# Low parts of some weight blocks from an accumulating DMA instead of VectorE, in a float32 decoder block

## The chip, the cores and the metric

The kernel runs on one core of one Trainium2 chip. The metric is the device time of one execution in microseconds (us).

## The reference

One decoder layer over 256 tokens with 2048 channels, all in float32:

```
h = x + 1/2 * SwiGLU_1(RMSNorm(h))                       d_ff = 5632
u = RMSNorm(h); proj = u @ W_in                           2048 -> 7168
    8 heads of a gated linear recurrence (HGRN2), and 8 channel groups of a short convolution
h = h + W_out(concat(group norms of both))
h = h + 1/2 * SwiGLU_2(RMSNorm(h))                       d_ff = 5632
h = h + sigmoid(RMSNorm(h) @ W_pg) * (p @ W_pe)
y = RMSNorm_final(h)
```

Nearly all of the work is in the weight matrices of the two feed-forward parts, of W_in, W_out and W_pg.

## The kernel before

**Two parts.** TensorE multiplies in the type float32r, which keeps fewer bits than float32. So each weight and each activation is kept as a high part (its float32r rounding) and a low part (what is left), and a product is made of three terms: high by high, high by low, low by high. `product` (L103) does this for one 128 x 128 weight block with two matmuls: the low part of the weights by the high part of 256 tokens, and the high part of the weights by both parts of the activations (512 columns). But for the first of an accumulation, the low part comes first (L106, then L107; for the first L107, then L109).

**Steps.** All weights pass through a list of 360 steps, each a block of at most 16 weight blocks of 128 x 128 (1 MB; 32 of the down steps have 12 blocks). Step numbers: 0 to 87 are gate and up of the first feed-forward by turns, 88 to 135 its down projection (three steps a column block, of 16, 16 and 12 weight blocks), 136 to 207 the mixer (W_in, then W_out), 208 to 295 gate and up of the second feed-forward, 296 to 343 its down projection, 344 to 359 the gate of the embedding.

**A step's weights.** `load` (L93) brings a step's weights into a buffer `raw` (three of them, RAW_BUFS) by a DMA that SyncE (SP) issues (L85). `split` (L98) takes the block in two halves of 8 (or 6) weight blocks each. For each half `split_piece` lets ScalarE (ACT) write the high part `hi` with an activation Copy (L90), and then VectorE (DVE) the low part `lo` = raw - hi (L91). There are four `hi` and four `lo` buffers of half a step each, so the parts of two steps are there at a time.

**Order.** The loop at L747 issues, for each step i: the load of step i + 3, the split of step i + 2, the matmuls of step i, its epilogue (L131 to L150, or L191 for a down step), and hooks of the mixer. A framework adds all semaphores and puts the instructions of each engine into one in-order queue, near to this program order. So the split of step i + 2 waits until the matmuls of step i are done with the same half of its `hi` and `lo` buffers; and the load of step i + 3 waits until the split of step i has read the buffer `raw` that it takes. Only the start (L712) has an order by hand. GpSimd (POOL) does nothing but a few memsets: constants, and in the mixer L278 and L288.

Of the kernel before, what the change touches and what calls it, by code (L numbers as in the profile page):

```python
# [7 lines left out]
F32 = mybir.dt.float32  # L8
F32R = mybir.dt.float32r
I32 = mybir.dt.int32  # L10
AF = mybir.ActivationFunctionType
ALU = mybir.AluOpType
PSUM = bass.MemoryType.PSUM

P = 128
T = 256            # tokens
T2 = 2 * T
NB = 16            # 128-wide blocks of d_model
NF = 44            # 128-wide blocks of d_ff
NH = 8             # heads, conv groups  # L20
EPS = 1e-6
MAGIC = float(0x5F3759DF)
STAGES = (2, 8, 32)  # each joins four blocks of this many tokens
HW = 2 * NH        # heads x windows of 128 tokens
NM = 64 + 192 * len(STAGES)

# columns of the packed per-channel vectors
C_FFN1, C_MIX, C_FFN2, C_PLE, C_FIN = 0, 16, 32, 48, 64
C_HN, C_CN, C_CW, C_LB, C_SEL, C_ID = 80, 81, 89, 113, 129, 139
NCST = C_ID + P  # L30
# [4 lines left out]


class Step:
    """One block of at most 16 x [128, 128] weights and what is done with it."""

    def __init__(self, src, nk, mm, epi=None):  # L40
        self.src, self.nk, self.mm, self.epi = src, nk, mm, epi
# [5 lines left out]
def kernel(  # L47
# [3 lines left out]
    nc = tc.nc  # L51
    V, A, TE = nc.vector, nc.scalar, nc.tensor
# [5 lines left out]

    hT = const.tile([P, NB, T], F32, name="hT")
    xs = const.tile([P, NB, T2], F32R, name="xs")  # L60
    cst = const.tile([P, NCST], F32, name="cst")
    ones = const.tile([P, P], F32, name="ones")
    ones_r = const.tile([P, P], F32R, name="ones_r")
    sel = const.tile([P, 2 * P], F32R, name="sel")
    acc = const.tile([P, T], F32, name="acc")
    rb = const.tile([P, T], F32, name="rb")
    rt = const.tile([P, 2], F32, name="rt")
    lb = const.tile([P, NH], F32, name="lb")
    oml = const.tile([P, NH], F32, name="oml")
    ident = cst[:, C_ID:C_ID + P]  # L70

    def tt(shape=(P, T), dtype=F32, tag="t", bufs=6):
        return tmp.tile(list(shape), dtype, tag=tag, name=tag, bufs=bufs)

# [1 line left out]
    def new_raw(s):  # L76
        s.raw = wpool.tile([P, NB, P], F32, tag="raw", name="raw", bufs=RAW_BUFS)

    def new_parts(s):
        s.half = s.nk // 2  # L80
        s.parts = [tuple(wpool.tile([P, NB // 2, P], F32R, tag=t, name=t) for t in ("hi", "lo"))
                   for _ in range(2)]
# [4 lines left out]
    def split_piece(s, a, b):  # L87
        hi, lo = s.parts[a // s.half]
        r, sl = s.raw[:, a:b, :], slice(a % s.half, a % s.half + b - a)
        A.activation(hi[:, sl, :], r, AF.Copy)  # L90
        V.tensor_tensor(lo[:, sl, :], r, hi[:, sl, :].bitcast(F32), ALU.subtract)  # L91
# [4 lines left out]
            load_piece(s, i * s.nk // n, (i + 1) * s.nk // n)  # L96

    def split(s):  # L98
        new_parts(s)
        for k0 in (0, s.half):  # L100
            split_piece(s, k0, k0 + s.half)

    def product(hi, lo, m, ps, first, last):  # L103
        """ps[:, :T] += hi.x_hi; ps[:, T:] += hi.x_lo + lo.x_hi"""
        if not first:
            TE.matmul(ps[:, T:], lo, m[:, :T], start=False, stop=False)  # L106
        TE.matmul(ps, hi, m, start=first, stop=last)  # L107
        if first:
            TE.matmul(ps[:, T:], lo, m[:, :T], start=False, stop=False)  # L109

    def product_one(hi, lo, m, ps, first, last):
        """ps[:, :T] += all three"""
        TE.matmul(ps[:, :T], lo, m[:, :T], start=first, stop=False)  # L113
        TE.matmul(ps[:, :T], hi, m[:, T:], start=False, stop=False)  # L114
        TE.matmul(ps[:, :T], hi, m[:, :T], start=False, stop=last)  # L115
# [11 lines left out]
    def new_ps():  # L127
        return psum.tile([P, T2], F32, tag="ps", name="ps")

# [1 line left out]
    def halves(ps):  # L131
        t = tt()
        A.activation(t, ps[:, T:], AF.Copy)  # L133
# [41 lines left out]
    def row_scale():  # L175
        ps = new_ps()
        TE.matmul(ps[:, :T], ones, acc, start=True, stop=True)
        v = tt()
        V.tensor_scalar(v, ps[:, :T], 1.0 / (NB * P), EPS, ALU.mult, ALU.add)
        rsqrt(rb, v)  # L180
# [4 lines left out]
    def token_scale(ps):  # L185
        v = tt(shape=(P, 2), tag="v2", bufs=1)
        for i in range(2):
            V.tensor_scalar(v[:, i:i + 1], ps[i][:, 0:1], 1.0 / (NB * P), EPS, ALU.mult, ALU.add)
        rsqrt(rt, v)
# [11 lines left out]
        prep(j, c_gain)  # L201
        square_sum(j)

# [1 line left out]
    steps = []  # L205

    def at(i, f):
# [14 lines left out]
    def ffn(wg, wu, wd, c_next):  # L222
# [13 lines left out]
        i0 = len(steps)  # L236
        for f in range(NF):
            add(wg[f], NB, *gemm_in(g_epi))
            add(wu[f], NB, *gemm_in(u_epi(f)))

        def open_hid(s):
            st["pool"] = ExitStack()
            pool = st["pool"].enter_context(tc.tile_pool(name="hidp", bufs=1))
            st["hid"] = pool.tile([P, NF, T2], F32R, name="hid")

# [14 lines left out]
        steps[-1].after = close_hid  # L260
        return i0

# [1 line left out]
    def mixer():  # L264
        i0 = len(steps)
        m = {}
# [1 line left out]
        def open_mix(s):  # L268
            st["pool"] = ExitStack()
            m1 = st["pool"].enter_context(tc.tile_pool(name="mix1", bufs=1))  # L270
            m["Y"] = m1.tile([P, NH, T], F32, name="Y")
            m["Q"] = m1.tile([P, NH, T], F32, name="Q")
            m["masks"] = m1.tile([P, NM], F32, name="masks")
# [6 lines left out]
            m2 = st["hg"].enter_context(tc.tile_pool(name="mix2", bufs=1))  # L280
            m["K"] = m2.tile([P, NH, T], F32, name="K")
            m["f"] = m2.tile([P, NH * T], F32, name="f")
            m["t12"] = m2.tile([P, NH * T // 8], F32, name="t12")
            m["tot"] = [m2.tile([P, NH * T // n], F32, name=f"tot{n}") for n in (*STAGES, P)]
            m["V"] = m2.tile([P, 2, NH, P], F32, name="V")
# [49 lines left out]
                V.tensor_tensor(windows(m["Q"][:, h, :]), q_of(h), windows(f), ALU.mult)  # L335
            return epi

        # Tokens are taken in blocks whose length grows. Within a block Q holds q_t times the decays
        # from the block's start through t, K holds k_s times those after s to the block's end, tot
        # the whole block's: a score between two blocks is then a product of rows, no factor of which  # L340
        # exceeds 1, and the blocks between come in with their tot.
        def pairs(a):
            return a.rearrange("p (b two) -> p b two", two=2)

# [55 lines left out]
        def stage_scores(si, h):  # L400
            L = STAGES[si]
            nb = P // (4 * L)
# [44 lines left out]
            return d  # L447

        def stat(key, g, d, first, last):
            """rows g and NH + g: the sum over the group's channels"""  # L450
            if first:
                st[key] = new_ps()
            e = sel[:, P - g:2 * P - g]
            TE.matmul(st[key][:, :T], e, d[:, :T], start=first, stop=False)
            TE.matmul(st[key][:, :T], e, d[:, T:], start=False, stop=last)

        def stat_done(key):
            v = tt()
            V.tensor_scalar(v, st[key][:, :T], 1.0 / P, EPS, ALU.mult, ALU.add)
            r = tt()  # L460
            rsqrt(r, v)
            # rows g hold the high parts, rows NH + g the low ones
            rs = st["rs", key] = m["m1"].tile([P, T], F32R, tag="rs", name="rs", bufs=2)
            A.activation(rs, r, AF.Copy)
            V.tensor_scalar(r, r, cst[:, C_SEL + 9:C_SEL + 10], None, ALU.mult)
            V.scalar_tensor_tensor(rs, rs.bitcast(F32), cst[:, C_SEL + 8:C_SEL + 9], r, ALU.mult, ALU.add)
# [4 lines left out]
            st["nr" + key, g] = d  # L471

        def norm(key, g, t):
            """t (in place) times its group's scale"""
            ps = new_ps()
            TE.matmul(ps[:, :T], ones_r, st["nr" + key, g], start=True, stop=True)
            V.tensor_tensor(t, ps[:, :T], t, ALU.mult)
# [45 lines left out]
        g0 = len(steps)  # L523
# [14 lines left out]
        k = c0 + 3  # L538
# [25 lines left out]
        for h in range(NH):  # L564
            at(k + 2 + h // 2, lambda h=h: norm_rows("o", h))
            at(k + 3 + h // 2, lambda h=h: norm("o", h, m["Q"][:, h, :]))
        assert k + 3 < g0  # a head's norm comes before its gate

        def conv_out(key, c):
            y = m["Y"][:, c, :]  # L570
# [3 lines left out]
        for c in range(NH):  # L574
            key = "y0" if c < 4 else "y1"
# [20 lines left out]
        steps[-1].after = close_mix  # L596
        return i0

# [1 line left out]
    def ple():  # L600
        i0 = len(steps)
        m = st["ple"] = {}
# [84 lines left out]
    scale_at = {i_f1 + 4, i_mix, i_f2, i_ple}  # L687
    late = []

# [1 line left out]
    # the first gate and up blocks side by side, so that both go on while x comes in  # L691
    nc.sync.dma_start(cst, cst_d)
    for i in range(2):
        steps[i].src = w_first[i]
# [17 lines left out]
    with tc.manual_schedule():  # L712
        for a, b in pieces:
            s = steps[a // 8]
# [15 lines left out]
        V.tensor_tensor(acc, acc, rb, ALU.add)  # L730

    def prologue():
        # the lower bound of the forget gate: the softmax's first row
        mx, e0, e1 = (tt(shape=(P, NH), tag="lbt", bufs=3) for _ in range(3))
        l0, l1 = cst[:, C_LB:C_LB + NH], cst[:, C_LB + NH:C_LB + 2 * NH]
        V.tensor_tensor(mx, l0, l1, ALU.max)
        V.tensor_tensor(e0, l0, mx, ALU.subtract)
        V.tensor_tensor(e1, l1, mx, ALU.subtract)
        A.activation(e0, e0, AF.Exp)
        A.activation(e1, e1, AF.Exp)  # L740
        V.tensor_tensor(e1, e0, e1, ALU.add)
        V.reciprocal(e1, e1)
        V.tensor_tensor(lb, e0, e1, ALU.mult)
        V.tensor_scalar(oml, lb, -1.0, 1.0, ALU.mult, ALU.add)
# [23 lines left out]
        if s.after:  # L768
            s.after(s)

# [1 line left out]
    m = st["ple"]  # L772
    ps = st["ts"]
    token_scale(ps)
# [3 lines left out]
    ps = new_ps()  # L778
# [66 lines left out]
```

## Time and profile before

| | us |
|---|---|
| two executions | 2048.87 and 2050.26, median 2049.57 |
| span of the profiled execution | 2047.5 |
| TensorE busy (matmul) | 2028.2 |
| VectorE busy | 1373.2 |
| ScalarE busy | 1004.2 |
| GpSimd busy | 2.9 |

The span goes from the first to the last instruction of the program. The profile does not say which of the two executions it is from; its span lies 1.4 to 2.8 us under their times, 2.1 us under the median. PE is TensorE's matmuls, PEld its weight loads, DVE VectorE, ACT ScalarE, POOL GpSimd, SP SyncE. The ends of matmuls are modelled and overlap, so their mean durations are longer than the pace at which they follow each other. "L90" is line 90 of the kernel.

### The profile page before, as it was taken

Reading aid. Unit: us, or ns where it says so; the run is one execution under the profiler, and the core shown is the slowest. Engines: PE = TensorE matmul, PEld = TensorE weight load, DVE = VectorE, ACT = ScalarE, POOL = GpSimd, SP = SyncE. Lnnn points to the kernel's source line nnn. Section 1 sums busy time; section 2 is a strip of 40 time slices with the busy share of each in tenths; the row PEclk is TensorE's granted clock in tenths of the full one; section 3 lists DMA queues with packets and bytes.
Section 4 is the critical chain, followed back from the end, with each engine's and each line's share of the span. In section 5 each row is a group of like instructions: output and inputs, shape, how many; then the busy total and the mean of one; then the engine's idle time right before and its main releaser. Section 6 shows DMA issues by size and latency. Waiting matters only on the chain.

```text
span 2047.5 us, 29112 instructions
## 1 busy us (share of the span) xinstructions
PE 2028.2 (99%) x11630; PEld 1774.8 (87%) x11630; DVE 1373.2 (67%) x2131; ACT 1004.2 (49%) x1510; POOL 2.9 (0%) x7
## 2 busy tenths in 40 slices
PE   8999999999999999999999999999999999999997
PEld 7888888888888888888888888888888888888986
DVE  8766666666555565689798776666666665555686
ACT  7444444444444444543566544444444444444463
POOL 0000000000000000000000000000000000000000
PEclk9999999999999999999999999999999999999998
DMA  7555555555555555544455555555555555555642
GB/s 250 205 188 188 191 193 188 186 185 182 184 190 190 185 199 190 189 165 145 144 168 186 187 185 192 192 188 185 185 186 187 190 186 188 177 195 187 237 164 84
DMA packets 55720, 378.00 MB, mean 185 GB/s; under 512 B 6176, under 2 KB 6432, under 8 KB 13728
## 3 DMA queue, kind: packets, MB, share of 16 engines
q1 hardware_dynamic: 55584, 376.14, 53.8%
q8 instruction: 91, 1.49, 0.3%
q14 instruction: 45, 0.37, 0.1%
HBM read 374.02 MB, written 2.10 MB: 184 GB/s over the span
## 4 chain that ended last, share of the span: by engine, by line
PE 98%; DMA 1%; DVE 1%; SPq 0%; issue 0%; ACT 0%; DVEq 0%; ACTq 0%
PE ps L107 61%; PE ps L106 29%; PE ps L109 2%; PE ps L405 1%; PE ps L306 1%; PE ps L307 1%; PE ps L308 1%; PE ps L114 1%; PE ps L115 1%; PE ps L113 1%; DMA hT<-xT 0%; DMA raw<-w1g 0%; PE ps L352 0%; DVE hg L782 0%; PE ps L438 0%
## 5 line engine op out<-in xcount | busy, mean ns | idle before, releaser
L107 PE MATMUL ps<-xs,hi 128*128 128x512 f32 x3824 | 1330.7, 394 | 5.9 <-DVE xs L154 5.9
L91 DVE TENSOR_TENSOR lo<-raw,hi 128x1024 fp32r<-128x1024 f32 (+2 forms) x724 | 865.1, 1195 | 637.4 <-ACT hi L90 636.6
L90 ACT ACTIVATE hi<-raw 128x1024 fp32r<-128x1024 f32 (+2 forms) x724 | 750.2, 1037 | 981.3 <-PE ps L107 624.2
L106 PE MATMUL ps<-xs,lo 128*128 128x256 f32 x3585 | 1002.3, 280 | 0.3 <-DVE lo L91 0.3
L107 PEld LDWEIGHTS ps<-xs,hi 128*128 128x128 f32 x3824 | 704.4, 188 | 156.2 <-ACT hi L90 5.9
L106 PEld LDWEIGHTS ps<-xs,lo 128*128 128x128 f32 x3585 | 672.3, 188 | 11.6 <-DVE lo L91 0.8
L107 PE MATMUL ps<-hid,hi 128*128 128x512 f32 x1320 | 461.3, 393 | 0.0
L106 PE MATMUL ps<-hid,lo 128*128 128x256 f32 x1290 | 364.5, 283 | 0.0
L107 PEld LDWEIGHTS ps<-hid,hi 128*128 128x128 f32 x1320 | 245.9, 188 | 54.8
L106 PEld LDWEIGHTS ps<-hid,lo 128*128 128x128 f32 x1290 | 242.5, 188 | 1.5
L140 DVE TENSOR_TENSOR t<-t,rb 128x256 f32<-128x256 f32 x231 | 97.5, 424 | 6.6
L134 DVE TENSOR_TENSOR t<-ps,t 128x256 f32<-128x256 f32 x239 | 99.8, 418 | 0.2 <-ACT t L133 0.2
L133 ACT ACTIVATE t<-ps 128x256 f32<-128x256 f32 x239 | 87.1, 366 | 0.9 <-DVE rb L162 0.9
L107 PE MATMUL ps<-mixout,hi 128*128 128x512 f32 x240 | 83.6, 397 | 0.0
L109 PE MATMUL ps<-xs,lo 128*128 128x256 f32 x239 | 67.8, 284 | 0.1
L106 PE MATMUL ps<-mixout,lo 128*128 128x256 f32 x225 | 63.1, 281 | 0.0
L109 PEld LDWEIGHTS ps<-xs,lo 128*128 128x128 f32 x239 | 45.1, 189 | 10.1 <-DVE lo L91 1.0
L107 PEld LDWEIGHTS ps<-mixout,hi 128*128 128x128 f32 x240 | 44.1, 188 | 9.5
L145 ACT ACTIVATE s<-t 128x256 f32<-128x256 f32 x112 | 45.0, 402 | 0.6 <-DVE t L140 0.6
L106 PEld LDWEIGHTS ps<-mixout,lo 128*128 128x128 f32 x225 | 42.2, 188 | 0.9 <-ACT mixout L149 0.2
L232 DVE TENSOR_TENSOR t<-t 128x256 f32<-128x256 f32 x88 | 37.3, 424 | 2.9
L150 DVE TENSOR_TENSOR hid<-t,hid 128x256 fp32r<-128x256 f32 x88 | 36.7, 418 | 0.1
(177 smaller groups left out, 931.9 us busy)
## 6 DMA issues: line engine op xcount, KB each, us to landing
raw<-w_in SPq DMA_DIRECT2D x48, 1024.0 KB, 4.9
raw<-w2g SPq DMA_DIRECT2D x44, 1024.0 KB, 4.8
raw<-w2u SPq DMA_DIRECT2D x44, 1024.0 KB, 4.8
raw<-w1u SPq DMA_DIRECT2D x43, 1024.0 KB, 4.8
raw<-w1g SPq DMA_DIRECT2D x42, 1024.0 KB, 4.8
raw<-w1d SPq DMA_DIRECT2D x32, 1024.0 KB, 4.9
raw<-w2d SPq DMA_DIRECT2D x32, 1024.0 KB, 4.9
raw<-w_out SPq DMA_DIRECT2D x16, 1024.0 KB, 4.8
```

What stands on the lines that cost most here:

```text
L90: A.activation(hi[:, sl, :], r, AF.Copy)
L91: V.tensor_tensor(lo[:, sl, :], r, hi[:, sl, :].bitcast(F32), ALU.subtract)
L106: TE.matmul(ps[:, T:], lo, m[:, :T], start=False, stop=False)
L107: TE.matmul(ps, hi, m, start=first, stop=last)
L109: TE.matmul(ps[:, T:], lo, m[:, :T], start=False, stop=False)
L113: TE.matmul(ps[:, :T], lo, m[:, :T], start=first, stop=False)
L133: A.activation(t, ps[:, T:], AF.Copy)
L134: V.tensor_tensor(t, ps[:, :T], t, ALU.add)
L140: V.tensor_tensor(dst, t, rb, ALU.mult)
L145: A.activation(s, src, AF.Sigmoid)
L150: V.tensor_tensor(dst[:, T:], src, dst[:, :T].bitcast(F32), ALU.subtract)
L232: V.tensor_tensor(u, u, st["g"], ALU.mult)
```

## The change

In each step whose number leaves a remainder of 3 when divided by 4 (3, 7, ... 359: 90 steps), the second half gets its low part in another way. ScalarE writes `hi` as before, then a second activation writes `lo` = -hi; then a DMA issued by GpSimd adds `raw` onto `lo`. The first half of these steps, and both halves of all others, are split as before. Nothing else changes but that comments are taken out (line numbers ahead of `split` stay).

```diff
     def split(s):
         new_parts(s)
-        for k0 in (0, s.half):
-            split_piece(s, k0, k0 + s.half)
+        split_piece(s, 0, s.half)
+        if steps.index(s) % 4 != 3:
+            split_piece(s, s.half, s.nk)
+            return
+        hi, lo = s.parts[1]
+        r = s.raw[:, s.half:s.nk, :]
+        A.activation(hi[:, :s.half, :], r, AF.Copy)
+        A.activation(lo[:, :s.half, :], hi[:, :s.half, :].bitcast(F32), AF.Copy, scale=-1.0)
+        nc.gpsimd.dma_start(lo[:, :s.half, :], r, accum_op=ALU.add)
```

## Rows read from the trace of the kernel before

**Rows 1.** The page's engine part: busy us, share of the span, instructions.
```profile
PE 2028.2 (99%) x11630; PEld 1774.8 (87%) x11630; DVE 1373.2 (67%) x2131; ACT 1004.2 (49%) x1510; POOL 2.9 (0%) x7
```

**Rows 2.** The page's chain that ended last: share of the span by engine.
```profile
PE 98%; DMA 1%; DVE 1%; SPq 0%; issue 0%; ACT 0%; DVEq 0%; ACTq 0%
```

**Rows 3.** The waits of PE, whole span: us in total, times, longest.
```profile
PE ps L107 <- DVE xs L154: 5.9, 1, 5.9
PE ps L779 <- DVE t L777: 2.8, 1, 2.8
PE ps L183 <- ACT t L654: 1.5, 1, 1.5
...
```

**Rows 4.** Windows: busy us (instructions) by engine, granted PE clock, DMA share, GB/s.
```profile
1170.00:1675.00 505.00, 505.00 (x2899) 441.09 (x2898) 342.40 (x507) 244.48 (x364) 0.00 (x0) 1.00 0.55 188
```

**Rows 5.** Groups by shape, whole span: count | busy us, mean ns | idle before.
```profile
L90 ACT ACTIVATE hi<-raw 128x1024 fp32r<-128x1024 f32 x652 | 691.1, 1060 | 890.5 <-PE ps L107 542.9 <-issue 303.0 <-PE ps L308 23.0
...
L90 ACT ACTIVATE hi<-raw 128x768 fp32r<-128x768 f32 x64 | 54.2, 846 | 90.0 <-PE ps L107 81.3 <-PE ps L115 5.8 <-issue 2.9
...
L91 DVE TENSOR_TENSOR lo<-raw,hi 128x1024 fp32r<-128x1024 f32 x652 | 798.3, 1225 | 581.8 <-ACT hi L90 581.4
...
L91 DVE TENSOR_TENSOR lo<-raw,hi 128x768 fp32r<-128x768 f32 x64 | 61.3, 958 | 54.6 <-ACT hi L90 54.4
```

**Rows 6.** Groups of ACT in the first 197 us.
```profile
L90 ACT ACTIVATE hi<-raw 128x1024 fp32r<-128x1024 f32 (+1 forms) x74 | 74.6, 1012 | 83.0 <-PE ps L107 43.8 <-issue 35.9 <-DMA raw<-w1u 1.4
```

**Rows 7.** Timeline of ACT, 197 to 215: start us, us, what [idle before].
```profile
200.19 1.06 ACT L90 ACTIVATE hi<-raw 128x1024 fp32r<-128x1024 f32 x1 [1.45 <-PE ps L107]
201.16 0.36 ACT L133 ACTIVATE t<-ps 128x256 f32<-128x256 f32 x1
202.99 1.06 ACT L90 ACTIVATE hi<-raw 128x1024 fp32r<-128x1024 f32 x1 [1.47 <-issue]
...
205.80 1.06 ACT L90 ACTIVATE hi<-raw 128x1024 fp32r<-128x1024 f32 x1 [1.45 <-PE ps L107]
...
208.59 1.06 ACT L90 ACTIVATE hi<-raw 128x1024 fp32r<-128x1024 f32 x1 [1.46 <-issue]
...
214.20 1.06 ACT L90 ACTIVATE hi<-raw 128x1024 fp32r<-128x1024 f32 x1 [1.47 <-issue]
```

**Rows 8.** Timeline of PEld, 207.5 to 209: start us, us, what.
```profile
208.47 0.19 PEld L106 LDWEIGHTS ps<-xs,lo 128*128 128x128 f32 x1
```

**Rows 9.** Timeline of DVE, 199 to 209.
```profile
201.29 1.23 DVE L91 TENSOR_TENSOR lo<-raw,hi 128x1024 fp32r<-128x1024 f32 x1 [1.25 <-ACT hi L90]
...
202.43 0.42 DVE L134 TENSOR_TENSOR t<-ps,t 128x256 f32<-128x256 f32 x1
```

**Rows 10.** Timeline of SP's queue, 190 to 225.
```profile
202.54 0.33 SPq L85 DMA_DIRECT2D raw<-w1g  x1
208.14 0.33 SPq L85 DMA_DIRECT2D raw<-w1u  x1
```

**Rows 11.** Groups of ACT in the first 513 us.
```profile
L90 ACT ACTIVATE hi<-raw 128x1024 fp32r<-128x1024 f32 (+1 forms) x187 | 194.1, 1039 | 248.0 <-PE ps L107 127.1 <-issue 117.7 <-DMA raw<-w1u 1.4
```

**Rows 12.** Timeline of ACT, 512 to 524.
```profile
514.18 1.06 ACT L90 ACTIVATE hi<-raw 128x1024 fp32r<-128x1024 f32 x1 [1.75 <-PE ps L107]
...
521.13 0.84 ACT L90 ACTIVATE hi<-raw 128x768 fp32r<-128x768 f32 x1 [1.47 <-PE ps L107]
```

**Rows 13.** DMA issues: what, queue, count, KB each, median us from issue to landing.
```profile
raw<-w1u SPq DMA_DIRECT2D x43, 1024.0 KB, 4.8
...
wpe<-w_pe SPq DMA_DIRECT2D x2, 1024.0 KB, 7.7
...
out_dram<-hg SPq DMA_DIRECT2D x1, 512.0 KB, 2.8
```

**Rows 14.** Timeline of POOL, whole span (the longest of its instructions).
```profile
750.25 2.67 POOL L288 MEMSET S<- 128x3072 f32 x1
```

## The prediction

> **What bounds the kernel now.** I read the engines' busy times first: the matmuls are busy 99% of the span, VectorE 67%, ScalarE 49%, and GpSimd has seven instructions in all [rows 1]. A busy share alone can hide waits, so the chain of waits comes next: 98% of it is TensorE, VectorE and the DMAs have 1% each [rows 2]. TensorE's own waits agree: the three largest are 5.9, 2.8 and 1.5 us, one occurrence each [rows 3], together 10.2 us, all at the start or the end. Last the clock: in a long stretch of the second feed-forward it is 1.00, the level of 2.4 GHz, with TensorE busy for 505.00 of 505 us [rows 4]. So TensorE sets the end nearly everywhere, and work taken from VectorE is worth nothing by itself. What matters is whether the new way delivers the low part before TensorE asks for it.
>
> **What goes.** 90 subtractions on VectorE: 82 of 1.225 us in full steps and 8 of 0.958 us in the steps with 12 weight blocks [rows 5], 100.5 + 7.7 = 108 us of 1373. None of it is on the chain [rows 2]; I count 0.
>
> **What comes on ScalarE.** 90 negations. Their shapes are those of the high parts, so they cost what L90 costs: 82 x 1.060 + 8 x 0.846 = 94 us [rows 5], ScalarE then 1098 us, 54% of the span. What lies behind each in ScalarE's queue is seen at step 35, an affected one: 74 high parts stand before 197 us [rows 6], that is 8 small pieces of steps 0 and 1 and 2 x 33 halves of steps 2 to 34, so the row at 200.19 is the second half of step 35 [rows 7]. Behind it comes the epilogue's copy L133 (201.16), then the next high part at 202.99, before which ScalarE was idle for 1.47 us. A negation of 1.06 us fits into that idle time. L133 comes 1.06 us later, but VectorE, which then no longer does the subtraction of 1.23 us from 201.29 on, takes up the copy's result at about 202.6 instead of 202.43 [rows 9]: a delay of 0.2 us in an epilogue for which TensorE does not wait. Cost 0; without the idle time, 1.06 us of delay to a high part that has some 6 us in hand, so still 0.
>
> **What comes as a wait.** Now the low part of a second half lands by DMA, and the first matmul of that half (L106) waits for it; behind that one stands all of TensorE's queue, so a late landing costs its whole lateness, 1 for 1. The time in hand for step 35: the high part ends at 201.25; a hand-over between engines takes 0.04 us (VectorE starts at 201.29) [rows 7, 9], counted twice; with the negation that makes 201.25 + 0.04 + 1.06 + 0.04 = 202.39 for the issue. The high part at 208.59 is the first half of step 37, which may start when TensorE is done with the first half of step 35 [rows 7]; the weight load just before it, at 208.47 [rows 8], is where TensorE takes the low part of the second half. In hand: 208.47 - 202.39 = 6.1 us. I take this for 82 of the 90 steps.
>
> The other 8 follow a step of 12 weight blocks (every third affected step of the down projections), so TensorE comes round sooner. For step 91, the second half of which starts at 514.18 (187 high parts before 513 us [rows 11]: 8 + 2 x 89 + the first half of step 91), the issue is at 515.24 + 0.04 + 1.06 + 0.04 = 516.38 and the first half of step 93 at 521.13 [rows 12]; less the same 0.12 us, 521.01. In hand: 4.6 us.
>
> With X as the time from issue to landing: **time = 2049.6 + 82 x (X - 6.1 if above 0) + 8 x (X - 4.6 if above 0)**.
>
> **The size of X.** No row shows an accumulating DMA, or any DMA from GpSimd's queue. From below: 512 KB out of this memory take 2.8 us [rows 13]. From above: two loads of 1024 KB issued one behind the other take 7.7 us each [rows 13], and GpSimd's longest instruction is 2.67 us against 0.33 us of SP's issue [rows 10, 14]: were an issue on GpSimd that long, X = 7.7 + 2.67 - 0.33 = 10.0 us. The sum has two operands of 512 KB, so 1024 KB are read: the nearest row is the load of 1024 KB, 4.8 us from issue to landing [rows 13], and that is what I take. The 16 DMA engines are free for it: the load of the step before was issued 5.6 us earlier (208.14 - 202.54 is the spacing [rows 10]) and has landed after 4.8, and the next cannot go out before this DMA has read the buffer.
>
> At 4.8 us the 82 steps have 1.3 us to spare and the 8 lose 0.2 us each, 1.6 us in all.
>
> The Trainium skill has a price (DMA: Bandwidth & Descriptors, Anatomy of one DMA): about 2.0 us fixed and the bytes at 436 GB/s, for a DMA from GpSimd; no run here shows it. With both operands counted that is an estimate of 4.4 us, also inside both times in hand, and the sum would be 2049.6.
>
> **What moves.** The buffer `raw` is now held until the DMA has landed. The load of step 38, issued at 202.54 after VectorE's subtraction [rows 9, 10], goes out at 202.39 + 4.8 = 207.2; beside the next load (208.14) it takes up to 7.7 us and lands by 214.9. The first half of step 38 started at 214.20 [rows 7], so ScalarE may wait 0.7 us. TensorE starts step 38 three steps after 205.80, at 222.6, and a half is split in 1.06 + 0.04 + 1.23 = 2.3 us: a load that lands by 220.2 costs nothing. So the load can be issued as late as 212.5, X up to 10.1: cost 0 in the whole range of X. SP's later loads are queued behind this wait, with the same time in hand. On GpSimd's queue stand only the memsets of the mixer (2.67 us, near 750 us [rows 14]): 0.
>
> **Sum.** On the span: 2047.5 + 1.6 = 2049.1; the median lies 2.1 above the span of the profiled execution, so 2051.2, near 2051 us.
>
> **Rivals.**
> *The DMA lands after TensorE asks (slower).* Its place is the first L106 of the second half of each affected step. It decides from X = 6.1 on in the 82 steps, and the time leaves 2% (41 us; about what a measurement of this kernel can tell from no change) at X = 6.4. For it: neither the operation nor a DMA from GpSimd's queue is in any row, and a sum has to read its target as well. Against it: the 1024 KB row is 1.6 us under 6.4. At 7.7 us it costs 82 x 1.6 + 8 x 3.1 = 156 us: 2206 us. At 10.0 us, 82 x 3.9 + 8 x 5.4 = 363 us: 2413.
> *GpSimd's queue alone is a little slower than SP's (just slower).* If the same 1024 KB take 1.7 us longer on it, X = 6.5: 82 x 0.4 + 8 x 1.9 = 48 us, 2098 us. No row speaks for or against this pace. A table of the Trainium skill speaks for it (DMA: Bandwidth & Descriptors, Bandwidth): 1 MB issued from GpSimd keeps the DMA engines busy for 6.15 us; no run here shows it, and it would be over the 6.1 us in hand before the issue is counted.
> *VectorE's relief shows (faster).* It could only come out of TensorE's waits, 10.2 us in the rows [rows 3], and these are at the start and the end, where at most one affected step lies: 2039 at the very best, still within 2%.
> *ScalarE's 94 us show.* This takes a stretch in which it has no idle time before the high parts; in rows 7 it has 1.45 us before each. Within 2%.
>
> **How the numbers follow.** Hidden, or nearly (X up to 6.4): 0.57, and I give its time, 2051, with a range of its own of 2045 to 2090. GpSimd's queue a little slower: 0.10. A landing well behind: 0.31, of which some 0.15 beyond 7.7 us. Faster by over 2%: 0.02, for what I have not seen. So faster 0.02, within 2% 0.57, slower 0.41. The range goes from 2044 to the 2206 of the 7.7 us row; it leaves out the landings near 10 us.
>
> **What would show it.** Right: TensorE's waits still hold no group on the low part; DMA issues on GpSimd's queue of 512 KB with a median landing under 6 us; SP's loads after affected steps 4 to 5 us later; ScalarE near 1098 us, VectorE near 1265. Wrong: a wait of TensorE (L106) for the DMA into `lo`, some 82 to 90 times, or a median landing over 6.4 us. A drop of the granted clock from 1.00 in the affected stretches would also show that TensorE pauses.

## The result, and the profile after

The changed kernel takes 2068.32 us (median of two executions, 2067.84 and 2068.81) against 2049.57 us: a ratio of 1.0092 with a 95% interval of 1.0062 to 1.0121. It is slower by 18.75 us, which is within 2% and inside the range given; the likeliest case said 1.6 us, so most of the loss has to be explained. The profiled execution took 2068.81 us with a span of 2067.0 us, 19.5 us over the span of before.

The page of the kernel after, its engine part and its DMA queues. Lines from `product` on are numbered 8 higher than before: L114 and L115 are the matmuls L106 and L107, L117 is L109, and L141 is the epilogue's copy L133.

```profile
PE 2035.3 (98%) x11630; PEld 1775.2 (86%) x11630; DVE 1279.8 (62%) x2041; ACT 1087.8 (53%) x1600; POOL 80.5 (4%) x97
...
q1 hardware_dynamic: 55584, 376.14, 50.6%
q0 software_dynamic: 12960, 46.14, 11.8%
q8 instruction: 91, 1.49, 0.3%
```

Against [rows 1] VectorE does 93 us less and ScalarE 84 us more (an engine's busy time counts overlaps of its instructions once; the instructions taken away and added make 108 and 93 us). The 90 new DMAs are queue q0.

The DMA issues after (KB each, median us to landing), then the waits of PE after (us in total, times, longest):

```profile
raw<-w1u SPq DMA_DIRECT2D x43, 1024.0 KB, 6.4
...
lo<-raw POOLq DMA_DIRECT2D x82, 512.0 KB, 4.6
...
lo<-raw POOLq DMA_DIRECT2D x8, 384.0 KB, 3.9
```

```profile
PE ps L117 <- DMA lo<-raw: 4.4, 3, 1.8
PE ps L114 <- DMA lo<-raw: 4.4, 4, 2.9
...
PE ps L121 <- DMA lo<-raw: 1.6, 1, 1.6
```

TensorE's matmuls now wait for the DMA into `lo`: 10.4 us, but only in 8 places, not in 82 or 90. Shorter waits show on the weight loads. Of the group of 16 below, four are places already counted; the other 12 are of 0.2 to 0.5 us, so there are some 20 places in all.

```profile
PEld ps L114 <- DMA lo<-raw: 10.1, 16, 3.2
```

The median landing is 4.6 us, a little under the 4.8 us of the forecast. So the question is what is special about the places.

The timeline of ACT after around step 35, the answer to [rows 7], and the DMA on POOL and the loads of SP beside it:

```profile
205.20 1.06 ACT L107 ACTIVATE hi<-raw 128x1024 fp32r<-128x1024 f32 x1 [1.45 <-PE ps L115]
206.17 0.36 ACT L141 ACTIVATE t<-ps 128x256 f32<-128x256 f32 x1
206.43 1.05 ACT L108 ACTIVATE lo<-hi 128x1024 fp32r<-128x1024 f32 x1
...
213.54 1.06 ACT L90 ACTIVATE hi<-raw 128x1024 fp32r<-128x1024 f32 x1 [1.47 <-PE ps L115]
```

```profile
207.78 0.86 POOL L109 DMA_DIRECT2D lo<-raw  x1 [21.54 <-ACT lo L108]
```

```profile
212.41 0.33 SPq L85 DMA_DIRECT2D raw<-w1g  x1
213.09 0.33 SPq L85 DMA_DIRECT2D raw<-w1u  x1
```

In this ordinary step everything is hidden. The negation ends at 207.48, GpSimd starts at 207.78, and the held load goes out at 212.41, just after the sum has landed (4.50 us after its issue, in the table of packets below); the first half of step 37 starts at 213.54, where TensorE passes to the second half of step 35. About 1.1 us are left.

Where the 19.5 us come from is read by laying the starts of the same instruction side by side: the second-half high part of a step, before and after, from the two timelines of ACT (us; the last column is the difference):

```
step   before     after   difference
   3    22.56     23.13      0.57
  11    65.63     70.80      5.17
  91   514.18    518.82      4.64
 139   762.28    768.63      6.35
 195  1110.77   1116.62      5.85
 211  1201.39   1215.68     14.29
 299  1694.85   1711.33     16.48
 343  1920.92   1939.86     18.94
 359  2021.02   2039.95     18.94
```

The start loses 5.2 us, the first gate and up steps nothing, the first down projection 1.7, the mixer up to W_out nothing, the 16 steps of W_out 8.4, the second gate and up steps 2.2, the second down projection 2.5. The same kind of step costs nothing in the first feed-forward and something in the second.

W_out first: PE, ACT and POOL around the start of step 199, after.

```profile
1142.76 1.06 ACT L107 ACTIVATE hi<-raw 128x1024 fp32r<-128x1024 f32 x1 [1.01 <-PE ps L115]
```

```profile
1145.33 0.86 POOL L109 DMA_DIRECT2D lo<-raw  x1 [24.84 <-DVE hT L208]
```

```profile
1147.96 0.63 PE L115 MATMUL ps<-mixout,hi 128*128 128x512 f32 x2
1149.90 0.39 PE L117 MATMUL ps<-mixout,lo 128*128 128x256 f32 x1 [1.31 <-DMA lo<-raw]
```

TensorE waits at L117, the first product of the step (in the last step of W_out, which goes through `product_one`, this is L121). `order` in W_out's `mm` is weight blocks 8 to 15, then 0 to 7: the half that the DMA serves is consumed first there.

The clock adds to the two longest pauses. Windows after, then the same two windows before (the column after POOL is the granted PE clock):

```profile
33.10:36.50 3.40, 3.40 (x12) 2.84 (x11) 1.81 (x2) 0.00 (x0) 0.00 (x0) 0.50 0.97 328
1125.30:1128.70 3.40, 3.40 (x13) 2.92 (x12) 0.96 (x3) 1.06 (x3) 0.00 (x0) 0.51 0.92 313
```

```profile
33.10:36.50 3.40, 3.40 (x21) 3.00 (x20) 2.90 (x3) 1.06 (x1) 0.00 (x0) 1.00 0.81 270
1125.30:1128.70 3.40, 3.40 (x21) 2.95 (x21) 1.96 (x3) 2.39 (x5) 0.00 (x0) 1.00 0.90 308
```

About 1 us after TensorE's waits at the start (2.9 us) and at the first affected step of W_out (1.8 us) the granted clock is 0.50, the level of 1.2 GHz, for 3.4 us, and 12 or 13 matmuls are done instead of 21. That gives away some 1.7 us more each time: 3.58 us are lost at that step of W_out, 1.59 to 1.68 at each of the three that follow, where the clock stays at 1.00.

### The profile page after: what moved, and what is told of

Read it like the earlier page. It is cut to its first block, busy times and chain, and to the rows that moved or that the text cites. A ratio compares the mean times of both kernels' runs of the same rounds, so it can differ in the third digit from the quotient of the medians.

```text
span 2067.0 us, 29571 instructions
## 1 busy us (share of the span) xinstructions
PE 2035.3 (98%) x11630; PEld 1775.2 (86%) x11630; DVE 1279.8 (62%) x2041; ACT 1087.8 (53%) x1600; POOL 80.5 (4%) x97
## 5 line engine op out<-in xcount | busy, mean ns | idle before, releaser
L115 PE MATMUL ps<-xs,hi 128*128 128x512 f32 x3824 | 1332.5, 394 | 5.7 <-DVE xs L162 5.7
L91 DVE TENSOR_TENSOR lo<-raw,hi 128x1024 fp32r<-128x1024 f32 (+2 forms) x634 | 756.9, 1194 | 620.5 <-ACT hi L90 619.1
L90 ACT ACTIVATE hi<-raw 128x1024 fp32r<-128x1024 f32 (+2 forms) x634 | 655.2, 1034 | 774.0 <-PE ps L115 619.4
L114 PE MATMUL ps<-xs,lo 128*128 128x256 f32 x3585 | 1003.0, 280 | 4.5 <-DMA lo<-raw 3.3
L115 PEld LDWEIGHTS ps<-xs,hi 128*128 128x128 f32 x3824 | 704.3, 188 | 155.4 <-ACT hi L90 5.7
L114 PEld LDWEIGHTS ps<-xs,lo 128*128 128x128 f32 x3585 | 672.8, 188 | 19.0 <-DMA lo<-raw 5.8
L115 PE MATMUL ps<-hid,hi 128*128 128x512 f32 x1320 | 461.7, 393 | 0.0
L114 PE MATMUL ps<-hid,lo 128*128 128x256 f32 x1290 | 365.5, 283 | 1.7 <-DMA lo<-raw 1.1
L115 PEld LDWEIGHTS ps<-hid,hi 128*128 128x128 f32 x1320 | 246.0, 188 | 54.2
L114 PEld LDWEIGHTS ps<-hid,lo 128*128 128x128 f32 x1290 | 242.5, 188 | 5.7 <-DMA lo<-raw 4.3
L107 ACT ACTIVATE hi<-raw 128x1024 fp32r<-128x1024 f32 (+1 forms) x90 | 93.7, 1041 | 124.6 <-PE ps L115 118.4
L109 POOL DMA_DIRECT2D lo<-raw x90 | 77.6, 862 | 1955.9 <-ACT lo L108 1415.4
L108 ACT ACTIVATE lo<-hi 128x1024 fp32r<-128x1024 f32 (+1 forms) x90 | 93.0, 1033 | 0.6
L141 ACT ACTIVATE t<-ps 128x256 f32<-128x256 f32 x239 | 86.6, 364 | 0.0
L115 PE MATMUL ps<-mixout,hi 128*128 128x512 f32 x240 | 85.1, 402 | 0.0
L117 PE MATMUL ps<-xs,lo 128*128 128x256 f32 x239 | 67.1, 281 | 0.2 <-DVE lo L91 0.2
L114 PE MATMUL ps<-mixout,lo 128*128 128x256 f32 x225 | 63.8, 284 | 0.0
L117 PEld LDWEIGHTS ps<-xs,lo 128*128 128x128 f32 x239 | 45.0, 188 | 10.7 <-DVE lo L91 1.1
L115 PEld LDWEIGHTS ps<-mixout,hi 128*128 128x128 f32 x240 | 44.9, 191 | 9.9
```

The source lines that it names most:

```text
L107: A.activation(hi[:, :s.half, :], r, AF.Copy)
L108: A.activation(lo[:, :s.half, :], hi[:, :s.half, :].bitcast(F32), AF.Copy, scale=-1.0)
L109: nc.gpsimd.dma_start(lo[:, :s.half, :], r, accum_op=ALU.add)
```

## The experiments

All runs are compared with the kernel before on the same chip. Line numbers move by a few with each edit.

**ScalarE's part alone (neg_dve).** The negation stays, VectorE does the sum, GpSimd nothing.

```diff
-        nc.gpsimd.dma_start(lo[:, :s.half, :], r, accum_op=ALU.add)
+        V.tensor_tensor(lo[:, :s.half, :], r, lo[:, :s.half, :].bitcast(F32), ALU.add)
```

> ScalarE negates as in the change, but VectorE adds raw onto lo; there is no DMA on GpSimd's queue. Theory (the loss is late landings alone): no wait of TensorE, 2049 to 2051 us. Rival (ScalarE's 93 us more, or the later epilogues behind the negation, hold something up): most of the 18.7 us stays, over 2060 us.

Measured: 2050.18 us, ratio 1.0005 (0.9996 to 1.0013). TensorE has the waits of the start and the end and two of 1.0 and 0.5 us, none on a negated part. ScalarE's 93 us and the later epilogues cost nothing that can be measured; the loss belongs to the DMA.

**The other half in W_out (wout_first).** In the four affected steps of W_out the DMA serves the half that is consumed second.

```diff
+            dma_half = 0 if 192 <= i < 208 else 1
```

> As the change, but in the four affected steps of W_out the DMA serves the first half of the block. Theory (W_out's products take the second half first, so a DMA there has half a step less in hand): the four waits at the first product of W_out's steps go, 8.4 us less, span near 2058.6 and time near 2060 us. Rival (W_out loses through its loads, which take 7 to 8 us there, or through ScalarE): the four waits stay at the start of the steps or come at their middle, time near 2068 us.

Measured: 2058.29 us, ratio 1.0047 (1.0034 to 1.0060), span 2057.8. The waits of PE in this run:

```profile
PE ps L118 <- DMA lo<-raw: 5.4, 10, 1.7
```

The groups of L117 and L121, the first products, are gone; 9.2 us of span go with them, where 8.4 were expected. Laid side by side with before as above, W_out loses nothing (the difference is 2.65 us at step 191 and 2.67 at step 207), so its 8.4 us are gone. The near agreement of the sum hides two other differences: the start loses 1.7 us instead of 5.2, because TensorE's wait there was 1.7 us and the clock stayed at 1.00 after it, and the second gate and up steps lose 4.4 us instead of 2.2. So the order of the halves was W_out's loss, not its loads and not ScalarE.

**Two steps earlier (residue1).** Steps 1, 5, 9, ... are affected. The reason for this run lies in the DMA packets of the trace. In the kernel after, nearly every DMA of q0 in the first gate and up steps lands after 4.5 us, but in the second ones after 4.56 to 5.97 us, although (at steps 223 and 227) the load before has landed. What is there is a fetch of instructions (queue q8, one packet of 16 KB, 0.9 to 1.5 us long there): its period is four steps too. The packets of four DMAs, times from the issue:

```
step   fetch on q8            last packet of q0   longest packet   landing
  35   over at 0.06 us             4.20 us           0.36 us       4.50 us
  55   over before the issue       4.19              0.36          4.54
 227   0.50 to 1.78 us             5.43              1.43          5.78
 235   0.35 to 1.79                5.59              1.66          5.87
```

The first packet of a sum starts 1.44 us after the issue. At step 227 all but five of the 144 packets have ended by 4.20 us, as at step 35; one packet has taken 1.43 us, and the last four full ones then end one by one, 0.31 us apart, until 5.43 us. So one engine's share is 1.2 us behind, and the landing waits for it. That this is the engine with the fetch is inferred: the trace does not name a packet's engine. Over the second gate and up steps the sum lands up to 1.4 us late, mostly the more the later the fetch ends: where it is over at 1.20 us, the landing is 4.58; where at 1.91 us, 5.97.

```diff
-        if steps.index(s) % 4 != 3:
+        if steps.index(s) % 4 != 1:
```

> As the change, but steps 1, 5, 9, ... (remainder 1) are affected. Theory (in the second feed-forward a 16 KB fetch of instructions falls 0.5 us behind each DMA and keeps one DMA engine 1.3 us back; both have a period of 4 steps): moved by two steps the landings in the second gate and up steps are 4.5 us as in the first ones, the start loses nothing, W_out and the steps behind a short one lose as before (8.4 and 8 x 0.4 us): 2060 to 2063 us. Rival (the slower landings belong to the second feed-forward, its buffers or its loads): landings there stay 5 to 6 us, 2063 to 2066 us.

Measured: 2069.33 us, ratio 1.0097 (1.0084 to 1.0111). The time was expected 6 to 9 us lower, yet the fetches behave as the theory says: in the second gate and up steps the landings are 4.48 to 5.13 us with a median of 4.52 (after: 5.37), no fetch meets one of them, and the difference to before stays at 11.2 us from step 207 to step 301. The affected steps are up steps, with the same loads, in both runs. So it is the fetch and not the stage. The start loses 0.3 us, W_out 8.1, the steps behind short ones some 0.35 us each. Two places that the expectation did not have take 9.1 us: step 121, behind a short step, with a fetch and a landing of 6.30 us (2.1 us), and step 345 (7.0 us). Of step 345, the loads on SP's queue, the DMA and the matmul that waits:

```profile
1943.83 0.90 SPq L622 DMA_DIRECT2D wpe<-w_pe  x2
```

```profile
1946.16 0.86 POOL L109 DMA_DIRECT2D lo<-raw  x1 [19.50 <-ACT t L177]
```

```profile
1957.53 0.58 PE L114 MATMUL ps<-xs,lo 128*128 128x256 f32 x1 [5.26 <-DMA lo<-raw]
```

```profile
1957.30:1960.70 3.40, 3.17 (x10) 2.78 (x11) 0.00 (x0) 0.00 (x0) 0.00 (x0) 0.50 0.60 186
```

Two loads of 1 MB of embedding weights went out 2 us earlier; the second lands at 1957.25 and the sum, of half the size, at 1957.49, after 11.3 us. From 1957.27 on the clock is at 0.50 for 3.4 us. That the loads are the cause is read from this coincidence; they were not moved in a run of their own.

**Only where there is time (covered).** As wout_first, and no DMA in step 3 or in the steps that follow a short step.

```diff
+        if i % 4 == 3 and i > 3 and not (88 <= i < 136 and (i - 88) % 3 == 0) and not (296 <= i < 344 and (i - 296) % 3 == 0):
```

> As the change, but no DMA in step 3 and in the steps that follow a short step, and the first half in W_out: 81 DMAs are left. Theory (lateness only where there is less than 5 us in hand, and the fetch in the second feed-forward): 2.2 us are left there, near 2052 us. Rival (each DMA costs something wherever it stands, 0.2 us of 18.7 us): 81 of 90 parts are left, near 2066 us.

Measured: 2053.64 us, ratio 1.0020 (1.0011 to 1.0029), span 2052.5. The 81 DMAs that are left do not carry their share; of the 5 us of span, some 1.1 are the start, 0.6 lie in the first down projection, and 3.3 in the second gate and up steps, where the fetches are (the mixer gives a little back). No DMA stands in the start here, so its 1.1 us are not a DMA's. The theory's 2052 was 1.6 us low.

**Only where there is time, away from the fetches (covered1).** The same with remainder 1, and without step 345.

```diff
+        if i % 4 == 1 and i != 345 and not (88 <= i < 136 and (i - 88) % 3 == 0) and not (296 <= i < 344 and (i - 296) % 3 == 0):
```

> As the run with remainder 1, but without the DMA in the steps that follow a short step and in step 345, and with the first half in W_out: 80 DMAs are left. Theory (every loss of that run has its place: short steps, W_out, a fetch of instructions in step 121, the 2 MB of embedding weights in flight at step 345): nothing is left but 0.3 us of the start, 2049 to 2051 us, landings 4.5 us everywhere. Rival (there is a cost per DMA that these places only hide): 2053 us or more.

Measured: 2050.38 us against 2050.20, ratio 1.0000 (0.9991 to 1.0009). Its DMA issues and its waits of PE, all there are:

```profile
lo<-raw POOLq DMA_DIRECT2D x72, 512.0 KB, 4.5
...
lo<-raw POOLq DMA_DIRECT2D x8, 384.0 KB, 3.9
```

```profile
PE ps L119 <- DVE xs L166: 5.7, 1, 5.7
PE ps L791 <- DVE t L789: 2.8, 1, 2.8
PE ps L118 <- DVE lo L91: 1.7, 1, 1.7
PE ps L195 <- ACT t L666: 1.5, 1, 1.5
```

The profiled execution has a span of 2049.1 us, 1.6 over before; 1.8 us of it are there by step 5, ahead of the first sum that TensorE needs, and nothing is added from there to the end. One weight load waits 0.3 us for a sum, at step 321, where a fetch makes the landing 5.75 us. So 80 accumulating DMAs cost nothing that can be measured when each has its time, and 96 us fewer on VectorE (80 subtractions at [rows 5]) gain nothing. The interval leaves room for some 0.02 us a DMA, a tenth of the 0.2 us that the whole loss would be when shared out.

**A copy instead of a sum (plain_copy).**

```diff
-        nc.gpsimd.dma_start(lo[:, :s.half, :], r, accum_op=ALU.add)
+        nc.gpsimd.dma_start(lo[:, :s.half, :], r)
```

> The DMA copies raw over lo and adds nothing, so the low part of these halves is raw itself and the negation is lost. Theory (a sum reads both operands, 1024 KB for 512 KB written, and the engines' reading sets its pace): the packets' time falls to about half, 1.4 of 2.7 us, and the landing from 4.5 to 3.1 to 3.3 us; the short-step waits go. Rival (the queue's fixed time and the writing set it): landings stay near 4.5 us.

Measured in one execution: 2052.19 us. No matmul waits on the DMA; one weight load does, 0.6 us in W_out. Its queue and issues:

```profile
q0 software_dynamic: 12960, 46.14, 6.2%
...
lo<-raw POOLq DMA_DIRECT2D x82, 512.0 KB, 2.9
...
lo<-raw POOLq DMA_DIRECT2D x8, 384.0 KB, 2.6
```

The packets of a copy take 0.062 x 2050.4 / 90 = 1.41 us of each engine, those of a sum 0.118 x 2067.0 / 90 = 2.71 us, and a load of 1024 KB some 2.9 (0.506 x 2067.0 us for 376 MB). So the packets of a sum take nearly as long as those of a load of twice its size, which is what the forecast took for it. The landing of the copy, 2.9 us, is below the 3.1 to 3.3 expected. The run takes away the second operand and the addition together, so it does not show which of the two the time goes to. GpSimd's instruction is shorter too: 0.53 us for a copy, 0.86 for a sum. In the second gate and up steps, where a fetch meets every one, the copies land after 3.8 to 4.2 us: the fetch delays a copy as well.

**Every second step (every2).** Both remainders at once, 179 DMAs.

```diff
-        if steps.index(s) % 4 != 3:
+        if steps.index(s) % 2 != 1:
```

> Every second step is affected (remainders 1 and 3). Theory (the losses of the two placements add up, each at its place: W_out 16, short steps 6, start 4.5, fetches 4, step 345 7 us): 2085 to 2095 us, and the steps between without a wait. Rival (with a DMA in every second step the loads of 1 MB, sent out late and in pairs, run into the next sum): landings over 5 us in plain gate and up steps, over 2120 us.

Measured in one execution: 2086.92 us. The median landing of 512 KB is still 4.5 us. Its waits of PE on the DMA:

```profile
PE ps L114 <- DMA lo<-raw: 12.6, 13, 4.9
...
PE ps L117 <- DMA lo<-raw: 9.6, 7, 1.8
...
PE ps L121 <- DMA lo<-raw: 1.6, 1, 1.6
```

Eight affected steps of W_out have their wait at the first product (L117, and L121 in the last step, which goes through `product_one`); with remainder 3 alone it was four. W_out loses 13.0 us where 16 were expected: its first wait is 1.75 us, as in the kernel after, but here the clock stays at 1.00 behind it. Twice the DMAs, some twice the loss (37.6 us of span, against 19.5 and 20.1), at the same kinds of places, and no general slowdown from loads that are sent out late.

## Why the prediction was right or wrong

*TensorE sets the end, VectorE's relief is worth nothing.* Right: covered1 takes it away and gains nothing.

*ScalarE's negations cost 0.* Right. They take 93 us (94 were counted), and neg_dve is within 0.05% of before. One detail differs: the epilogue's copy was put between the high part and the negation, so the epilogue is hardly delayed and the negation starts 0.17 us after the high part, not 0.04.

*X = 4.8 us.* Near, and the row it was taken from fits: the packets of a sum take 2.71 us of an engine and those of the 1024 KB load 2.9. From the issue X is 4.5 us, 0.3 less than forecast. That the sum lands when it was forecast to is partly luck: at step 35 the issue comes 0.38 us later than reckoned (0.17 and 0.29 us at the two hand-overs instead of 0.04 each), and the shorter landing makes up for it. The estimate of 4.4 us from the Trainium skill (DMA: Bandwidth & Descriptors, Anatomy of one DMA) was 0.1 us short of what is measured from the issue. The rival by the 1 MB row of its table (DMA: Bandwidth & Descriptors, Bandwidth; 6.15 us) did not come about: from the first to the last packet a sum takes 2.8 us (1.44 to 4.20).

*6.1 us in hand for 82 steps.* This is the step that failed. It was read at one step of the first gate and up stage and carried to all others. It holds there (the measured rest is 1.1 us against 1.3) and in most of the mixer. It does not hold in W_out, where the order of the halves is turned round: the rows of step 199 after have 1148.6 - 1145.33 = 3.3 us from the issue to TensorE's arrival, and 4 of the 82 steps make 8.4 of the 19.5 us of span, over two fifths of the loss. Nor does it hold at step 3, in the start with its order by hand: TensorE is there 3.6 us after the issue (at 29.20, the issue at 25.58), so 4.5 us would have been 0.9 us late already, and the sum landed after 6.4. A load was in flight until 4.0 us after the issue and a fetch until 1.1; which of them held the sum up was not tested. The start loses 5.2 us, 2.9 of them the wait and 1.7 the clock. `order` stood in the kernel and the start in the text; neither was asked what it does to the time in hand.

*8 steps behind a short step lose 0.2 us each.* The right place with a size a little small: 0.3 to 0.4 us where no fetch meets them, for the hand-over of 0.29 us.

*X is one number.* The range of X in one trace was left out: a fetch of instructions makes it 4.6 to 6 us in the second gate and up steps (2.2 us lost there) and 5.5 us at step 299 (1.3 us), and other loads 11.3 us once in residue1. With 1.1 us to spare such steps turn from free to late.

*The buffer `raw` held longer costs 0.* Right: w1u's median landing goes from 4.8 to 6.4 us, since two loads now run side by side, and in covered1 and every2 TensorE has no wait behind it (ScalarE has one of 1.6 us in covered1).

*The rival "lands after TensorE asks".* Its mechanism and its place (the first matmul that needs the half) are what happened, in some 20 places instead of 82 or 90, and so within 2%. The price, the lateness 1 for 1, was too low: in W_out waits of 1.3, 1.3 and 1.6 us cost 1.6, 1.6 and 1.7, and one of 1.8 us, with the clock at 0.50 behind it, cost 3.6. The drop of the granted clock, named as a sign of pauses, came twice and carries some 3.4 us of the loss. That the time stayed within 2% rests on X under 5 us, for which the forecast had its reason; that the places with less in hand, which it did not look for, were so few is luck.

## What to carry to other kernels

The time in hand of a transfer is a property of each place where it is used: list the consumers and their order (which half first, which step is short, what the start and the changes of stage have in flight) and take it at each of them, not at a typical one. Work moved off an engine that does not set the end gained nothing here, and lost in the few places with the least time in hand; with those left out the move was free, and still worth nothing. Where something periodic is placed in a schedule of equal steps, look for other periodic traffic, such as instruction fetches, with the same period: a shift by two steps removed every collision of one stage, and brought a new one at step 121 that cost 2.1 us.

## What had not been expected of the hardware

A fetch of 16 KB of instructions, one packet of 0.9 to 1.5 us, delayed a DMA of 144 packets by 0.1 to 1.4 us when it ended 1.2 to 1.9 us after the issue (4.5 us became up to 5.97), and not at all at step 243, where it was over after 0.64 us. Nearly all packets ended in time; the landing came after the few that were held up.

A sum by DMA costs packets' time of 2.71 us against 1.41 for a copy of the same 512 KB, and its issue on GpSimd 0.86 us against 0.53.

A pause of TensorE was followed by 3.4 us at a granted clock of 0.50 in some places and not in others. In the kernel after, the clock fell about 1 us after the end of the pauses of 2.9 us at the start and 1.8 us in W_out, and not at the three of 1.3 to 1.6 us that followed there. In residue1 it fell 1.1 us after a pause of 1.8 us in W_out, and 0.3 us before the end of that of 5.3 us at step 345, but not at one of 1.9 us at step 121. In every2 it fell before the end of a pause of 4.9 us at step 345, but not at one of 1.75 us in W_out, nor in wout_first at one of 1.7 us at the start. The same pause at the first affected step of W_out was thus followed by a drop in two runs and not in a third. So neither the length of a pause nor its place says it, and what else does stays open.
